# Where the operands of the last matrix product are made: eleven pairs beside one projection, or spread over three

## The chip, the cores and the metric

The kernel runs on one core of one Trainium2 chip. The metric is device time in microseconds (us) of one execution; the median of several executions is compared. A second number, the span, comes from a profiled execution and reaches from its first to its last instruction.

## What is computed

The reference is one layer of a diffusion block over 1024 tokens of width 1024, in fp32:

```python
h = modulate(rmsnorm(x, g_mix), mod[0], mod[1])
p = h @ w_in                       # f_f, f_b, i, q, og, u, v, ga, gb
o_a = HGRN2 scans of p, both directions (512 wide), gated by silu(og)
o_b = spatial gating of gelu(u), gelu(v)   (512 wide)
merged = sigmoid(ga) * (o_a @ w_pa) + sigmoid(gb) * (o_b @ w_pb)
x = x + mod[2] * (merged @ w_o)
h2 = modulate(rmsnorm(x, g_ffn), mod[3], mod[4])
a, b = split(h2 @ w_up)            # 2816 columns each
x = x + mod[5] * ((silu(a) * b) @ w_down)
out = rmsnorm(x, g_final)
```

`mod` are six vectors of 1024 numbers, each `silu(c) @ w_mod[:, j] + b_mod[j]`. `mod[5]`, the last gate, scales the columns of the last product; the kernel multiplies it into `w_down` instead, before the product.

## The kernel before

**Arithmetic.** Every fp32 operand of a large product is split into a high part (ScalarE, ACT, copies it to the reduced format, L92) and a low part (VectorE, DVE, subtracts, L93); three matmuls (L121 to L123) replace one. The input projection, `w_up` and `w_down` use a seven-product Strassen scheme on top, so sums and differences of blocks of both sides are made as well.

**Stages, in order.** Input projection in 18 pairs of column blocks (loop over `PAIRS`, n = 0 to 17); product with `w_pb` (8 column blocks m, L828); scans of four heads; product with `w_pa` (8 blocks, `branch(w_pa, ...)`, L958); `w_o`; `w_up` in 22 pairs (loop from L1033); `w_down` in six segments.

**The vectors of `mod`.** `mod_sum(j)` loads eight blocks of `w_mod` (512 KB each, into the four `raw` buffers that all weights use) and accumulates them with eight DVE instructions (L668, L670). `mod_rows(j, a, dst)` loads the bias row, sums over the partitions with two matmuls (L681) and adds (L682): `dst` is then the vector, the same in every partition. For j = 5 both happen in the `w_up` loop, after m = 2 and m = 4.

**`down_operands(i)`**, the subject of the change, makes what `w_down` needs for the i-th of eleven pairs of row blocks, a set: two loads of 512 KB (`rawd`, two buffers, L1018 and L1019); two multiplications by `m5` on GpSimd (POOL, L1020 and L1021); four differences on DVE (L1024 to L1028, three of them into `t` tiles, which are `gl` buffers); seven splits on ACT and DVE (`od`); seven stores of 512 KB to DRAM (L1031), issued on SyncE's queue (SP), the queue of nearly all loads. The `w_down` stage loads the results again (`so`). The eleven sets are placed in the `w_up` loop after m = 5, 6, 8, 9, 11, 12, 14, 15, 16, 18, 19.

**Memory.** One pool, `slots`, has NS = 31 tiles of 4 KB in each partition and serves nearly every long-lived tile: operands, `m5`, `moda`, the `od` tiles, the scans' tiles. In the `w_up` stage the right-hand operands G are 28 of them (seven names by four). The `gl` tag has six buffers: the gates `g` and the partial results `pb` of `w_pb` and `w_pa`, and the `t` tiles.

**Order.** Outside the first stage nobody writes the order of an engine's queue by hand. A planner walks all instructions with a time model: the one that comes first in the program goes first when it is ready, and a later one takes its place when it is not. So a position in the program is a priority, not a time. On the chip each queue is in order: ACT, DVE, POOL, PE (TensorE) and SP each stand still behind an instruction that waits.

Of the kernel before, what the change touches and what calls it, by code (L numbers as in the profile page):

```python
# [8 lines left out]
F32 = mybir.dt.float32  # L9
# [3 lines left out]
ALU = mybir.AluOpType  # L13
# [21 lines left out]
H0, H1 = slice(0, HALF), slice(HALF, T)  # L35
# [3 lines left out]
def blk(i):  # L39
    return slice(i * P, (i + 1) * P)  # L40
# [3 lines left out]
def block_kernel(ctx: ExitStack, tc: tile.TileContext,  # L44
# [32 lines left out]
    def gl_(name="gl"):  # L77
        return wp.tile([P, HALF], F32, name=name, tag="gl", bufs=6)
# [159 lines left out]
    def dtile(name, shape=(P, T)):  # L238
        return dram.tile(list(shape), F32, name=name)
# [3 lines left out]
    Id = [dtile(f"Id{t}", (P, HALF)) for t in range(TT)]  # L243
    Vd = [dtile(f"Vd{t}", (P, HALF)) for t in range(TT)]
    m2d = dtile("m2d")
    PBd = [dtile(f"PBd{m}") for m in range(KT)]
    X1d = [dtile(f"X1d{t}") for t in range(TT)]
    Gd = [dtile(f"Gd{m}", (P, 2, T)) for m in range(NFF // 2)]
# [143 lines left out]
    with tc.manual_schedule():  # L392
# [22 lines left out]
        a = mods_x(1)  # L415
# [245 lines left out]
    def mod_sum(j):  # L661

        a = slot("moda")
        for k in range(KT):
            raw = raw_()
            load(out=raw, in_=w_mod[blk(k), j * D:(j + 1) * D])
            if k == 0:
                dve.tensor_scalar(a, raw, sc[:, k, 0:1], None, op0=ALU.mult)  # L668
            else:
                dve.scalar_tensor_tensor(a, raw, sc[:, k, 0:1], a, op0=ALU.mult, op1=ALU.add)  # L670
        return a
# [62 lines left out]
    for n, (ka, fa, kb, fb) in enumerate(PAIRS):  # L734
        p_ = early[n] if n < len(early) else in_pair(n).head()
        if n == len(PAIRS) - 1:
            sg4 = slot("sg4", (P, 2, HALF))
            wsr, wsT = sg4[:, 0, :], sg4[:, 1, :]
            bsb = slot("bsb")[:, :HALF]
            load(out=wsr.rearrange("p (g s) -> p g s", s=P), in_=w_s[0].rearrange("g t s -> t g s"))  # L740
            load(out=bsb, in_=b_s.rearrange("a g t -> a (g t)").broadcast_to([P, HALF]))
        X, c12, c21, c22 = p_.rest(turn_ws if n == len(PAIRS) - 1 else None)
        if n == 0:
            with tc.issue_after(t_done.ins):
                for t in range(4):
                    vnorm(4 + t, vlate[t], dve)
        if ka[0] == "q":
            q = slot("q")
            act.copy(q[:, H0], X)
            pool.tensor_copy(q[:, H1], c12)  # L750
            for s, z in ((H0, c21), (H1, c22)):
                sg = gl_("sg")
                sig = after(lambda: act.activation(sg, z, AF.Sigmoid))
                pool.tensor_tensor(z, z, sg, op=ALU.mult)
                store(out=pd[kb][:, s], in_=z)
            table_use[0] = sig
            continue
        if ka[0] == "ff":
            e = ev_()
            zs = (e, c12, c21, c22)  # L760
            for z, src in zip(zs, (X, c12, c21, c22)):
                sig = after(lambda: act.activation(z, src, AF.Sigmoid))
            table_use[0] = sig
            gates(ka[1], zs, q)
        else:
            e = ev_()
            act.activation(e, X, fa)
            todo = ((ka, AF.Copy, H0, e), (ka, fa, H1, c12), (kb, fb, H0, c21), (kb, fb, H1, c22))
        for key, fn, s, z in (todo if ka[0] != "ff" else ()):
            if fn != AF.Copy:  # L770
                last_act = act.activation(z, z, fn)
            store(out=pd[key][:, s], in_=z)
        if n in (11, 13):
            ma = mod_sum({11: 3, 13: 4}[n])
        if n in (12, 14):
            mod_cols({12: 3, 14: 4}[n], ma)
        if n == 15:
            store(out=m2d, in_=mod_sum(2))
        if n == 7:
            act.activation(EA, EA, AF.Exp)  # L780
            E = EA.rearrange("p j (c i) -> p j c i", i=2)
            XA, GA, HA = (const.tile([P, 8, 8, 2], F32, name=nm) for nm in ("XA", "GA", "HA"))
            AP = const.tile([P, 8, 8], F32, name="AP")
            dve.memset(XA, 1.0)
            for dr in range(2):
                d_ = slice(4 * dr, 4 * dr + 4)
                a, b = (0, 1) if dr == 0 else (1, 0)
                Ea, Eb = E[:, d_, :, a], E[:, d_, :, b]
                X_ = XA[:, d_, :, 0]
                dve.tensor_tensor(X_, Ea, Eb, op=ALU.mult)  # L790
                dve.tensor_tensor(AP[:, d_, :], X_, X_, op=ALU.mult)
                dve.tensor_copy(GA[:, d_, :, a], Ea)
                dve.tensor_tensor(GA[:, d_, :, b], X_, Ea, op=ALU.mult)
                dve.tensor_copy(HA[:, d_, :, b], Eb)
                dve.tensor_tensor(HA[:, d_, :, a], X_, Eb, op=ALU.mult)
    dve.scalar_tensor_tensor(A2, modc[:, 4, :], 1.0, cols[:, C_GF:C_GF + 8], op0=ALU.add, op1=ALU.mult)


    V = [slot("V", (P, 2, HALF)) for _ in range(4)]
# [17 lines left out]
    def branch(w, m, src, gate, fin):  # L817
        o = wop(load_cols(w, m * P, 4))
        for h_ in range(2):
            g_ = gl_("g")  # L820
            load(out=g_, in_=pd[gate, m][:, HS[h_]])
            ps = psum()
            for k in range(4):
                mm3(ps, hl(o, blk(k)), hl(src[h_][k]), k == 0, k == 3)
            dve.tensor_tensor(g_, ps, g_, op=ALU.mult)
            fin(h_, g_)

    for m in range(KT):  # L828
        branch(w_pb, m, OB, "gb", lambda h_, g_: store(out=PBd[m][:, HS[h_]], in_=g_))

    scT = [slot(f"scT{d}", (P, NP, P)) for d in range(2)]
    for d in range(2):
# [119 lines left out]
    for m in range(KT):  # L952
        def fin(h_, g_):
            b_ = gl_("pb")
            load(out=b_, in_=PBd[m][:, HS[h_]])
            pool.tensor_tensor(g_, g_, b_, op=ALU.add)
            M[h_][m] = split_into(op_slot("M"), g_)
        branch(w_pa, m, OA, "ga", fin)  # L958
        if m == 3:
            mod_rows(2, ma, m2)  # L960

# [44 lines left out]
                combine(F0[k][0], zs[0], F0[k][1], zs[1], k, G)  # L1006

    SEG = [([0], [1])] + [([4 * i + 2, 4 * i + 3], [4 * i + 4, 4 * i + 5]) for i in range(5)]
    DPAIRS = [(ka, kb) for a, b in SEG for ka, kb in zip(a, b)]
    MADE_AT = {5 + 16 * i // 11: i for i in range(len(DPAIRS))}

    def down_operands(i):
        ka, kb = DPAIRS[i]
        ra, rb = (wp.tile([P, T], F32, name="rawd", tag="rawd", bufs=2) for _ in range(2))
        load(out=ra, in_=w_down[blk(ka), :])  # L1018
        load(out=rb, in_=w_down[blk(kb), :])  # L1019
        pool.tensor_tensor(ra, ra, m5, op=ALU.mult)  # L1020
        pool.tensor_tensor(rb, rb, m5, op=ALU.mult)  # L1021
        x11, x12, x21, x22 = ra[:, H0], ra[:, H1], rb[:, H0], rb[:, H1]
        t1, t3, t4 = (gl_("t") for _ in range(3))
        dve.tensor_tensor(t1, x12, x11, op=ALU.subtract)  # L1024
        dve.tensor_tensor(t3, x22, x12, op=ALU.subtract)
        t2 = x12
        dve.tensor_tensor(t2, x22, t1, op=ALU.subtract)
        dve.tensor_tensor(t4, x21, t2, op=ALU.subtract)  # L1028
        for nm, v in (("B11", x11), ("T1", t1), ("T3", t3), ("T2", t2), ("B22", x22), ("B21", x21), ("T4", t4)):
            o = split_into(op_slot("od"), v)  # L1030
            load(out=Od[nm, i], in_=o.bitcast(F32))  # L1031

    for m in range(NFF):  # L1033
        X, c12, c21, c22 = (early[m] if m < len(early) else up_pair(m).head()).rest()
        e = ev_()
        act.activation(e, X, AF.Silu)
        dve.tensor_tensor(e, e, c21, op=ALU.mult)
        store(out=Gd[m // 2][:, m % 2, H0], in_=e)
        act.activation(c12, c12, AF.Silu)
        pool.tensor_tensor(c12, c12, c22, op=ALU.mult)  # L1040
        store(out=Gd[m // 2][:, m % 2, H1], in_=c12)
        if m == 2:
            ma = mod_sum(5)
# [196 lines left out]
```

## Time and profile before

| what | us |
|---|---|
| median of 3 executions | 1568.43 |
| lowest, highest | 1560.66, 1570.03 |
| profiled execution, its own time | 1572.1 |
| its span | 1570.2 |
| PE, DVE, ACT, POOL busy in the span | 1459.1, 1178.9, 726.7, 684.1 |

In the trace the last input pairs run to about 580 us, `w_pb` to 632, the scans to 703, `w_pa` to 760, `w_o` and its norms to about 860 (the first `w_up` products overlap them), `w_up` to about 1346, `w_down` to the end. Busy times of stretches show how full each engine is; PE's matmuls are pipelined, so the number of matmuls in a stretch says more of its pace than its busy time.

### The profile page before, as it was taken

The numbers are of one execution on the slowest core, as the hardware profiler recorded it, in microseconds if no ns is written. First come the engines' busy times: TensorE is split into PE (matmuls) and PEld (weight loads), VectorE is DVE, ScalarE is ACT, GpSimd is POOL, SyncE is SP. The second block draws the span as 40 slices with busy tenths as digits, with TensorE's granted clock in tenths as the row PEclk, the third lists the DMA queues.
The fourth block names the chain that finished last, engine by engine and source line by source line (L and its number), as shares of the span: only waits on it lengthen the run. The fifth ranks groups of instructions, "written<-read, shape, count | busy, mean of one in ns | idle before, by whom it ended". The sixth has DMA issues, their size and how long they took to land. (4 is left out here: it accounts for less than half of the span.)

```text
span 1570.2 us, 19218 instructions
## 1 busy us (share of the span) xinstructions
PE 1459.1 (93%) x6574; PEld 1182.2 (75%) x6574; DVE 1178.9 (75%) x1642; ACT 726.7 (46%) x1214; POOL 684.1 (44%) x441
## 2 busy tenths in 40 slices
PE   6799979999999999999999899988888899999997
PEld 5677757777788787986888677766766688778886
DVE  5797898988867657775646997888988744578787
ACT  5345545676533331343254523433343334577645
POOL 2663564443233214343314555555564531444356
PEclk9899989999999999999999999999999899999999
DMA  9685302333677577623644263767677724599832
GB/s 304 221 295 161 93 27 81 130 126 114 209 240 227 176 257 270 237 81 119 230 148 161 67 194 115 253 235 268 243 258 256 273 87 141 188 343 355 300 121 107
DMA packets 210963, 302.78 MB, mean 193 GB/s; under 512 B 11857, under 2 KB 132274, under 8 KB 210866
## 3 DMA queue, kind: packets, MB, share of 16 engines
q1 hardware_dynamic: 185954, 253.84, 49.1%
q10 hardware_dynamic: 24912, 47.72, 8.2%
q8 instruction: 51, 0.84, 0.2%
q14 instruction: 46, 0.38, 0.1%
HBM read 211.34 MB, written 90.18 MB: 192 GB/s over the span
## 5 line engine op out<-in xcount | busy, mean ns | idle before, releaser
L93 DVE TENSOR_TENSOR op<-raw,op 128x512 fp32r<-128x512 f32 x200 | 180.5, 907 | 87.0 <-ACT op L92 86.1
L92 ACT CAST op<-raw 128x512 fp32r<-128x512 f32 x216 | 131.7, 620 | 169.7 <-PE acc L123 112.1
L121 PE MATMUL acc<-T,op 128*128 128x512 f32 x408 | 164.9, 405 | 22.4 <-DVE u L188 18.7
L121 PE MATMUL aux<-T,op 128*128 128x512 f32 x408 | 163.8, 402 | 19.1 <-DVE u L188 10.1
L93 DVE TENSOR_TENSOR op<-st,op 128x512 fp32r<-128x512 f32 x160 | 161.0, 1008 | 10.8 <-ACT op L92 9.2
L122 PE MATMUL acc<-T,op 128*128 128x512 f32 x408 | 164.8, 404 | 3.9 <-DVE T L93 3.8
L123 PE MATMUL acc<-T,op 128*128 128x512 f32 x408 | 163.8, 402 | 1.9 <-DVE op L93 1.9
L122 PE MATMUL aux<-T,op 128*128 128x512 f32 x408 | 162.7, 399 | 2.3 <-DVE T L93 2.3
L123 PE MATMUL aux<-T,op 128*128 128x512 f32 x408 | 161.9, 397 | 0.3 <-DVE op L93 0.3
L92 ACT CAST op<-st 128x512 fp32r<-128x512 f32 x160 | 97.9, 618 | 116.3 <-PE aux L123 37.2
L181 POOL TENSOR_TENSOR st<-raw 128x512 f32<-128x512 f32 x40 | 63.9, 1597 | 173.7 <-DMA raw<-in_w_in_dram 90.5
L121 PE MATMUL aux<-B,op 128*128 128x512 f32 x306 | 120.4, 394 | 10.1 <-DVE u L190 9.6
L195 POOL TENSOR_TENSOR st<-raw,st 128x512 f32<-128x512 f32 x40 | 59.3, 1482 | 159.8 <-DVE op L93 143.7
L121 PE MATMUL acc<-B,op 128*128 128x512 f32 x306 | 122.0, 399 | 6.3 <-DVE u L190 4.7
L122 PE MATMUL acc<-B,op 128*128 128x512 f32 x306 | 120.8, 395 | 0.0
L123 PE MATMUL acc<-B,op 128*128 128x512 f32 x306 | 120.6, 395 | 0.0
L123 PE MATMUL aux<-B,op 128*128 128x512 f32 x306 | 119.2, 390 | 0.6 <-DVE op L1155 0.4
L122 PE MATMUL aux<-B,op 128*128 128x512 f32 x306 | 119.4, 390 | 0.0
L121 PEld LDWEIGHTS acc<-T,op 128*128 128x128 f32 x408 | 79.3, 194 | 44.6 <-DVE u L188 21.9
L121 PEld LDWEIGHTS aux<-T,op 128*128 128x128 f32 x408 | 78.4, 192 | 41.0 <-DVE u L188 13.6
L122 PEld LDWEIGHTS acc<-T,op 128*128 128x128 f32 x408 | 79.8, 196 | 21.8 <-DVE T L93 5.4
L123 PEld LDWEIGHTS acc<-T,op 128*128 128x128 f32 x408 | 79.6, 195 | 19.2 <-DVE op L93 2.6
(365 smaller groups left out, 3601.7 us busy)
## 6 DMA issues: line engine op xcount, KB each, us to landing
raw<-in_w_in_dram SPq DMA_DIRECT2D x60, 512.0 KB, 4.9
raw<-in_w_up_dram SPq DMA_DIRECT2D x46, 512.0 KB, 4.2
OdT<-od SPq DMA_DIRECT2D x44, 512.0 KB, 3.6
so<-OdT SPq DMA_DIRECT2D x44, 512.0 KB, 5.6
OdB<-od SPq DMA_DIRECT2D x33, 512.0 KB, 3.5
so<-OdB SPq DMA_DIRECT2D x33, 512.0 KB, 6.0
raw<-in_w_mod_dram SPq DMA_DIRECT2D x32, 512.0 KB, 4.1
rawd<-in_w_down_dram SPq DMA_DIRECT2D x22, 512.0 KB, 5.2
```

The costliest lines, as they stand in the source:

```text
L92: (act.copy if hi_eng is act else hi_eng.tensor_copy)(h, v)
L93: t_last[0] = lo_eng.tensor_tensor(l, v, h.bitcast(F32), op=ALU.subtract)
L121: pe.matmul(ps, lh, rh, start=first, stop=False, skip_group_check=cont)
L122: pe.matmul(ps, lh, rl, start=False, stop=False, skip_group_check=cont)
L123: pe.matmul(ps, ll, rh, start=False, stop=last, skip_group_check=cont)
L181: pool.tensor_tensor(s1, a21, a22, op=ALU.add)
L195: pool.tensor_tensor(s4, a12, s2, op=ALU.subtract)
```

## The change

The last gate's vector is made in the input projection: `mod_sum(5)` after pair 16, `mod_rows` after pair 17, and the result stays in a slot and is also stored to DRAM (`m5d`). `down_operands` moves ahead of `w_pb`, takes the vector as an argument, and is called after m = 1 and 4 of `w_pb` (sets 0 and 1), after m = 1, 3 and 5 of `w_pa` (sets 2 to 4) and after m = 3, 6, 9, 12, 15 and 18 of `w_up` (sets 5 to 10). `last_gate()` loads the vector again for `w_pa` and for `w_up`. One of a set's two multiplications goes from POOL to DVE.

```diff
+    m5d = dtile("m5d")
...
-        if n in (11, 13):
-            ma = mod_sum({11: 3, 13: 4}[n])
+        if n in (11, 13, 16):
+            ma = mod_sum({11: 3, 13: 4, 16: 5}[n])
...
+        if n == 17:
+            m5 = slot("m5")
+            mod_rows(5, ma, m5)
+            store(out=m5d, in_=m5)
...
+    def last_gate():
+        z = slot("m5")
+        load(out=z, in_=m5d)
+        return z
+
+    def down_operands(i, m5):
...
+        dve.tensor_tensor(ra, ra, m5, op=ALU.mult)
+        pool.tensor_tensor(rb, rb, m5, op=ALU.mult)
...
         branch(w_pb, m, OB, "gb", lambda h_, g_: store(out=PBd[m][:, HS[h_]], in_=g_))
+        if m in (1, 4):
+            down_operands(m // 3, m5)
...
         branch(w_pa, m, OA, "ga", fin)
+        if m == 0:
+            m5 = last_gate()
+        if m in (1, 3, 5):
+            down_operands(2 + m // 2, m5)
...
-    MADE_AT = {5 + 16 * i // 11: i for i in range(len(DPAIRS))}
...
-        pool.tensor_tensor(ra, ra, m5, op=ALU.mult)
-        pool.tensor_tensor(rb, rb, m5, op=ALU.mult)
...
-        if m == 2:
-            ma = mod_sum(5)
-        if m == 4:
-            m5 = slot("m5")
-            mod_rows(5, ma, m5)
-        if m in MADE_AT:
-            down_operands(MADE_AT[m])
+        if m == 1:
+            m5 = last_gate()
+        if m >= 3 and m % 3 == 0 and m <= 18:
+            down_operands(4 + m // 3, m5)
```

## Rows read from the trace of the kernel before

**Rows 1.** Page: busy us (share of the span) and instructions, two engines

```profile
PE 1459.1 (93%) x6574; PEld 1182.2 (75%) x6574; DVE 1178.9 (75%) x1642; ACT 726.7 (46%) x1214; POOL 684.1 (44%) x441
```

**Rows 2.** Stretches, w_up: length, PE, PEld, DVE, ACT, POOL busy (instructions), PE clock, DMA, GB/s

```profile
880.00:900.00 20.00, 15.80 (x56) 11.18 (x54) 19.76 (x21) 11.23 (x20) 11.41 (x7) 0.83 0.19 56
900.00:918.94 18.94, 18.18 (x79) 14.72 (x80) 18.94 (x25) 6.15 (x11) 3.93 (x2) 1.00 0.63 198
...
968.56:996.72 28.16, 28.16 (x125) 23.29 (x125) 22.67 (x26) 10.88 (x20) 14.32 (x9) 1.00 0.57 198
...
1065.51:1237.59 172.08, 147.81 (x595) 116.32 (x594) 148.96 (x169) 67.39 (x120) 92.87 (x50) 0.94 0.73 256
1237.59:1254.77 17.18, 13.67 (x54) 10.82 (x53) 10.40 (x15) 5.54 (x10) 7.54 (x6) 0.90 0.86 307
1254.77:1273.58 18.81, 18.81 (x85) 15.58 (x84) 9.29 (x13) 5.73 (x11) 6.39 (x6) 1.00 0.30 92
```

**Rows 3.** POOL in order of time: ends of pairs (L1040), starts of sets (L1020)

```profile
968.56 1.30 POOL L1040 TENSOR_TENSOR m<-m,u 128x512 f32<-128x512 f32 x1
969.81 2.42 POOL L1020 TENSOR_TENSOR rawd<-rawd,m 128x1024 f32<-128x1024 f32 x1
...
1219.07 2.83 POOL L1020 TENSOR_TENSOR rawd<-rawd,m 128x1024 f32<-128x1024 f32 x1
...
1237.59 1.73 POOL L1040 TENSOR_TENSOR m<-m,u 128x512 f32<-128x512 f32 x1
```

**Rows 4.** The tile od: who waited for its stores (us, times), and stores' landing

```profile
  ACT od L92: 105.2, 49
...
DMA to landing us min/median/max: 2.6/3.6/8.2
```

**Rows 5.** DVE in order of time beside one POOL multiplication, within w_up

```profile
1149.37 1.17 DVE L1024 TENSOR_TENSOR t<-rawd 128x512 f32<-128x512 f32 x1
1150.46 2.89 DVE L93 TENSOR_TENSOR op<-st,op 128x512 fp32r<-128x512 f32 x1
1153.28 0.68 DVE L93 TENSOR_TENSOR od<-rawd,od 128x512 fp32r<-128x512 f32 x1
```

**Rows 6.** Groups by line and shape, 860 to 1300: busy us, mean ns, idle before

```profile
L670 DVE SCALAR_TENSOR_TENSOR moda<-raw,sc,moda 128x1024 f32<-128x1024 f32 x7 | 9.3, 1333 | 0.0
```

**Rows 7.** DVE in order of time, input projection: ends of pairs 10, 14 (L200)

```profile
441.04 0.68 DVE L200 TENSOR_TENSOR m<-aux,m 128x512 f32<-128x512 f32 x1
...
520.64 0.68 DVE L200 TENSOR_TENSOR m<-aux,m 128x512 f32<-128x512 f32 x1
```

**Rows 8.** Stretches from the last input pair to w_pa, columns as in Rows 2

```profile
560.00:580.00 20.00, 19.75 (x101) 16.63 (x100) 9.85 (x15) 7.12 (x12) 0.89 (x1) 1.00 0.86 263
580.00:610.00 30.00, 27.99 (x136) 21.68 (x135) 22.11 (x27) 6.72 (x11) 15.90 (x10) 1.00 0.71 247
610.00:650.00 40.00, 40.00 (x263) 34.96 (x262) 25.63 (x38) 8.28 (x16) 12.76 (x6) 1.00 0.99 356
650.00:703.00 53.00, 52.18 (x439) 46.88 (x438) 41.92 (x70) 21.96 (x42) 25.11 (x14) 1.00 0.26 92
703.00:760.00 57.00, 53.14 (x232) 41.74 (x231) 32.85 (x42) 18.57 (x32) 23.52 (x18) 0.97 0.44 145
```

**Rows 9.** Page: DMA issues: count, KB each, us to landing

```profile
OdT<-od SPq DMA_DIRECT2D x44, 512.0 KB, 3.6
...
rawd<-in_w_down_dram SPq DMA_DIRECT2D x22, 512.0 KB, 5.2
```

**Rows 10.** Waits from 600 to 640, three engines: us in total, times, longest

```profile
DVE g L825 <- DMA g<-gb: 7.2, 4, 3.2
...
POOL kd L847 <- DMA kin<-ki: 18.8, 2, 12.6
...
SPq L821 <- DMA PBd<-g: 20.6, 5, 11.9
```

**Rows 11.** Groups by line and shape, 580 to 640: columns as in Rows 6

```profile
L848 DVE TENSOR_TENSOR kx<-kin,XA 128x1024 f32<-128x1024 f32 x2 | 2.4, 1221 | 1.3 <-DMA kin<-ki 1.3
```

**Rows 12.** Waits from 700 to 770: DVE and SP, columns as in Rows 10

```profile
DVE g L825 <- DMA g<-ga: 6.0, 3, 3.2
...
SPq L821 <- POOL g L956: 36.3, 7, 29.7
```

More of the change, by code (lines that the diff above doesn't have):

```diff
@@ L796, in block_kernel @@
     dve.scalar_tensor_tensor(A2, modc[:, 4, :], 1.0, cols[:, C_GF:C_GF + 8], op0=ALU.add, op1=ALU.mult)
+    SEG = [([0], [1])] + [([4 * i + 2, 4 * i + 3], [4 * i + 4, 4 * i + 5]) for i in range(5)]
+    DPAIRS = [(ka, kb) for a, b in SEG for ka, kb in zip(a, b)]
+    def last_gate():
[3 more added lines that the diff above has]
+    def down_operands(i, m5):
+        ka, kb = DPAIRS[i]
+        ra, rb = (wp.tile([P, T], F32, name="rawd", tag="rawd", bufs=2) for _ in range(2))
+        load(out=ra, in_=w_down[blk(ka), :])
+        load(out=rb, in_=w_down[blk(kb), :])
+        dve.tensor_tensor(ra, ra, m5, op=ALU.mult)
+        pool.tensor_tensor(rb, rb, m5, op=ALU.mult)
+        x11, x12, x21, x22 = ra[:, H0], ra[:, H1], rb[:, H0], rb[:, H1]
+        t1, t3, t4 = (gl_("t") for _ in range(3))
+        dve.tensor_tensor(t1, x12, x11, op=ALU.subtract)
+        dve.tensor_tensor(t3, x22, x12, op=ALU.subtract)
+        t2 = x12
+        dve.tensor_tensor(t2, x22, t1, op=ALU.subtract)
+        dve.tensor_tensor(t4, x21, t2, op=ALU.subtract)
+        for nm, v in (("B11", x11), ("T1", t1), ("T3", t3), ("T2", t2), ("B22", x22), ("B21", x21), ("T4", t4)):
+            o = split_into(op_slot("od"), v)
+            load(out=Od[nm, i], in_=o.bitcast(F32))
     V = [slot("V", (P, 2, HALF)) for _ in range(4)]
@@ L1006, in block_kernel @@
                 combine(F0[k][0], zs[0], F0[k][1], zs[1], k, G)
-    SEG = [([0], [1])] + [([4 * i + 2, 4 * i + 3], [4 * i + 4, 4 * i + 5]) for i in range(5)]
-    DPAIRS = [(ka, kb) for a, b in SEG for ka, kb in zip(a, b)]
-    MADE_AT = {5 + 16 * i // 11: i for i in range(len(DPAIRS))}
[L1015 to L1019, printed above, removed]
-        pool.tensor_tensor(ra, ra, m5, op=ALU.mult)
-        pool.tensor_tensor(rb, rb, m5, op=ALU.mult)
[L1022 to L1031, printed above, removed]
     for m in range(NFF):
```

## Prediction

> **What bounds the kernel now.** I read the page's busy times first: PE 93%, DVE 75% [rows 1]. The average decides nothing, since the stages differ, so the stretches by stage come next. In `w_up` they tell the story. Once the sets are done, a pair takes 18.81 us, PE is busy throughout and DVE for 9.29 us. While sets are made, seven pairs take 172.08 us, 24.58 us each, DVE is busy 148.96 us, and the granted clock is 0.94 on average [rows 2]. POOL's order in time gives the rhythm: each pair carries one set. The first set starts at 969.81 us, right after the pair that ends at 968.56 us; the last at 1219.07 us, in the pair that ends at 1237.59 us, though the program places it four pairs later [rows 3]. So the planner pulls sets forward as soon as they are ready; what the text spaces, the queues pack.
>
> The price of a set follows. The eleven pairs from 968.56 to 1237.59 us take 269.0 us and carry eleven sets. At 18.81 us they would take 206.9. That is 62.1 us more; the next pair, 17.18 us, gives 1.6 back [rows 2, 3]. **60.5 us for eleven sets, 5.5 us each.** In DVE time a set costs (148.96 − 7 × 9.29) / 7 = 12.0 us [rows 2], so a pair with a set is 21.3 us of DVE work against 18.81 us of PE work. DVE is the bound there, and the remaining 3.3 us are waits: ACT stood 105.2 us before `od` casts, in 49 waits, until an `od` store had landed [rows 4]. G holds 28 of 31 slots and `m5` one; two are left for `od`.
>
> **The change part by part.** *Sets that leave `w_up`.* Five of eleven: −5 × 5.5 = −27.5 us, if the six that stay are again packed one to a pair. I count on that, since `m5` is read back early in the loop and nothing else holds the sets. Bounds: packed into the first pairs, where DVE is full (19.76 of 20 us, then 18.94 of 18.94) [rows 2], a set could cost its whole 12.0 us instead of 5.5, +6.5; spread out, see the second rival.
>
> *`mod_sum(5)` leaves `w_up`.* Seven accumulations of 1.33 us and one multiplication, some 10 us of DVE [rows 6], go from exactly that full stretch. I take 0, because set 5 (12.0 us) will move in; −10 is the bound if it doesn't.
>
> *`mod_sum(5)` in the input projection.* Four pairs from 441.04 to 520.64 us carry two such sums and take 79.6 us [rows 7]; without them 4 × 18.81 = 75.2 [rows 2]. So 2.2 us a sum: **+2.2** (0 to 4.4). Its eight loads of 512 KB share four `raw` buffers and SP's queue with the last weights; that is in the 2.2. The two matmuls and the bias load only change place. Before the last pair, `moda`, `sg4` and `bsb` and the scans' start state want four slots beside H's 28, one more than there are; the pair's first product frees four, so I take 0 (up to one product of seven, 2.7 us).
>
> *Reading `m5d` back.* A store and two loads of 512 KB, each landing in 3.6 to 5.2 us by the like rows [rows 9], off the path: 0. SP's wait for the vector's slot is the one place where loads could queue behind it.
>
> *The swap of one multiplication to DVE.* DVE pays 1.22 us for 128x1024 elements [rows 11], POOL is spared 2.83 us [rows 3]. Two-input DVE work beside a POOL multiplication is slow: the split at 1150.46 us takes 2.89 us, the next one alone 0.68 [rows 5]. If the spared POOL time gives such a delay back, DVE gains 2.21 and pays 1.22, −1.0; if not, +1.2. I take 0 a set, bounds −6 and +7 for the six sets of `w_up`. The Trainium skill (GPSIMD Engine Reference, Key points) says that GpSimd shares its SBUF interfaces with VectorE, with contention where a VectorE instruction has two SBUF inputs. The trace agrees; by this rule the swap would be the −6 end, by counting instructions the +7 end.
>
> *Two sets beside `w_pb`.* A set moves nine transfers of 512 KB [rows 9], 4.72 MB, at the 356 GB/s of the fullest stretch [rows 8] 13.3 us; two sets 26.5. From 560 to 703 us DMA has 51 us free and DVE 43 us [rows 8], against 26.5 and 24.0 needed: in sum it fits, lower bound 0. But from 610 to 650 us DMA is at 0.99 [rows 8], and its loads are wanted: POOL waits 18.8 us for `kin`, DVE 7.2 us for `gb` [rows 10]. Only 11.5 us of DMA time are free before 610 us, so up to 15 us of `w_pb`'s and the scans' loads land that much later, and PE, which is full there, has nothing else: upper bound 15. Queued behind an `od` store that waits for DVE stand, on SP, the `gb`, `kin` and `qin` loads. I take **+7**, about the middle, since today's waits don't reach PE.
>
> *Three sets beside `w_pa`.* DVE is busy 32.85 of 57 us [rows 8]; three sets make 68.9, 11.9 over. PE idles some 4 us there already, DMA is at 0.44 [rows 8], and sets may slip into `w_o`: lower bound 0. Upper bound 16.5, as dear as in `w_up`. I take **+7**.
>
> The sum: −27.5 + 2.2 + 7 + 7 = −11.3 us. Against the profiled execution, 1572.1 us (span 1570.2), that is 1560.8; that execution lay 3.7 above the median, so I forecast **1557** for the median.
>
> **The rivals.** *First, the moved sets are free.* The waits of ACT for landing stores [rows 4], 9.6 us a set, come from two free slots. Beside `w_pa`, OA holds 8 slots, M grows from 0 to 16, and three vectors take 3: 4 to 20 are free. If the slots, not DVE, set the price, both +7 vanish: −25.3, 1543 us. Against it: DVE alone is over PE's time. The Trainium skill (Perfetto Trace Analysis, Identifying Performance Opportunities) says that the same gap coming back on the engine that should be saturated can mean too little SBUF for the next tile. By that rule this rival is the case; the trace shows the gap once a pair, and DVE beside it.
>
> *Second, the six sets stay apart as written*, one to three pairs: 39.9 us of DVE against 56.4 of PE, so a set would cost perhaps 1 us. −60.5 + 6 + 2.2 + 14 = −38.3, 1530 us. Against it stands the last set that ran four pairs early [rows 3].
>
> *Third, DVE work costs the same wherever it goes*: five sets at 5.5 us again, +27.5. The gain is used up: +2.2, 1571 us. For it: DVE is busy 58 to 79% in those stages too [rows 8].
>
> *Fourth, slower: the `gl` buffers.* A set's `t` tiles hold three of six. A half block of `w_pa` holds two (`g`, `pb`); sixteen pass in 57 us, 3.6 us each, and loads already wait for buffers: SP 36.3 us for POOL's addition in `w_pa`, 20.6 us for the store in `w_pb`; DVE 6.0 us for `ga` [rows 8, 10, 12]. With half the buffers the pace halves while the `t` tiles are held, so a set costs half its hold. If it is held for as long as a set takes in `w_up`, 24.6 us, five sets cost 61.5: −27.5 + 2.2 + 61.5 = +36.2, 1605 us. It decides from a hold of 10 us on, where five halves are 25 us. Against it: a set needs only 12.0 us of DVE, and with free slots nothing stretches it.
>
> **How the numbers follow.** Chances: forecast 0.42 (its own range 1549 to 1565), first rival 0.17, second 0.11, third 0.18, fourth 0.12. The range 1536 to 1580 takes in the forecast, the first and the third rival and leaves out most of the second and of the fourth, 0.2 together. A measurement can tell about 1%, 15.7 us: faster is below 1552.7, slower above 1584.1. Faster: both first rivals and a quarter of the forecast, 0.38; slower: the fourth and a little more, 0.14; the same 0.48.
>
> **What would show it.** Right: in `w_up`, six pairs of about 24.6 us and the rest near 18.8, the stage 27 us shorter; `w_pb` with the scans and `w_pa` some 7 us longer each, PE waiting there for DVE or for `kin`; a third sum about 40 us after the last in the input projection. Wrong: the first rival shows as stages of the old length with five sets in them; the second as sets three pairs apart; the fourth as `ga` and `gb` loads that wait on SP, and PE on L825. The forecast falls first if the planner brings the moved sets somewhere else, into the scans above all, where DVE is busiest.

## The result, and the profile after

The changed kernel takes 1605.69 us (median of 4, 1602.6 to 1607.9) against 1568.11: the ratio is 1.0241, with an interval of 1.0213 to 1.0268. It is slower by 2.4%, where 1557 us was forecast; the time lies outside the range. The profiled execution spans 1601.6 us, 31.4 more than before.

The page's first part answers [rows 1]: PE has the same work, DVE 23 us less and POOL 35 us less, so the 31.4 us are not busy time of any engine added up.

```profile
PE 1459.0 (91%) x6574; PEld 1185.3 (74%) x6574; DVE 1155.9 (72%) x1653; ACT 726.7 (45%) x1214; POOL 649.2 (41%) x430
```

The stretches of the changed kernel, cut where its stages begin and end (columns as in [rows 2]), answer [rows 2, 8]: the end of the input projection, `w_pb`, the scans, `w_pa`, `w_o`, then three stretches of `w_up`.

```profile
500.00:570.00 70.00, 62.72 (x265) 50.40 (x264) 44.82 (x57) 21.31 (x37) 11.00 (x8) 0.95 0.70 218
591.50:655.00 63.50, 53.25 (x222) 43.65 (x223) 40.92 (x57) 16.14 (x28) 13.03 (x8) 0.89 0.76 273
655.00:743.50 88.50, 75.83 (x611) 68.02 (x609) 63.33 (x98) 28.21 (x55) 43.02 (x21) 0.92 0.54 203
743.50:831.00 87.50, 57.16 (x223) 42.99 (x223) 59.02 (x70) 27.45 (x49) 29.93 (x18) 0.86 0.57 204
831.00:925.00 94.00, 91.36 (x418) 75.17 (x417) 52.86 (x76) 39.44 (x69) 24.20 (x17) 1.00 0.58 207
1030.15:1140.24 110.09, 100.11 (x415) 80.75 (x414) 96.95 (x121) 45.59 (x82) 48.78 (x30) 0.95 0.79 272
1140.24:1154.72 14.48, 14.48 (x65) 12.00 (x64) 10.15 (x13) 5.45 (x10) 7.28 (x6) 1.00 0.68 228
1154.72:1344.90 190.18, 190.18 (x840) 157.48 (x840) 91.34 (x130) 60.80 (x102) 63.94 (x51) 1.00 0.28 85
```

`w_up` did what was hoped, and more. Once the sets are done, ten pairs take 19.0 us each with PE full; five pairs with sets take 22.0 us each. What it won was lost almost twice over elsewhere: beside the 222 to 223 matmuls of `w_pb` and of `w_pa` PE now stands idle 10 and 30 us, and no engine is full there on average. The tile `od` answers [rows 4]: ACT waits half as long for its stores, which land later.

```profile
  ACT od L92: 55.4, 27
...
DMA to landing us min/median/max: 2.6/4.7/8.4
```

The stage lengths of all kernels, in us of each profiled execution: from the first matmul on OB (`w_pb`) to the first on OA (`w_pa`), to the last on OA, to the last on M (`w_o`), and to the last store of `Gd` (`w_up`).

| kernel | V's first matmul at | `w_pb` and scans | `w_pa` | `w_o` | `w_up` | median | ratio (interval) |
|---|---|---|---|---|---|---|---|
| before | 576.8 | 121.8 | 55.5 | 91.3 | 499.1 | 1568.11 | 1 |
| after | 585.1 | 152.0 | 87.2 | 93.9 | 457.7 | 1605.69 | 1.0241 (1.0213 to 1.0268) |
| e1 vector only | 582.5 | 120.1 | 54.8 | 90.7 | 491.0 | 1562.55 | 0.9982 (0.9963 to 1.0) |
| e2 two sets by `w_pb` | 584.8 | 154.9 | 52.0 | 91.2 | 471.3 | 1581.53 | 1.0112 (1.0086 to 1.0138) |
| e3 three sets by `w_pa` | 580.2 | 118.9 | 86.7 | 96.5 | 472.3 | 1583.95 | 1.0126 (1.01 to 1.0152) |
| e4 own `t` buffers | 586.2 | 151.9 | 71.0 | 101.1 | 457.6 | 1595.95 | 1.0204 (1.017 to 1.0237) |
| e5 scans' loads first | 586.9 | 144.9 | 71.8 | 102.5 | 456.8 | 1589.71 | 1.0158 (1.0119 to 1.0197) |
| e6 low parts on POOL | 584.6 | 151.4 | 70.7 | 103.3 | 455.9 | 1594.1 | 1.0188 (1.015 to 1.0226) |
| e7 stores on ACT's queue | 582.5 | 151.1 | 75.6 | 95.9 | 457.7 | 1590.04 | 1.0159 (1.0121 to 1.0196) |
| e8 swap only | 572.4 | 120.6 | 53.3 | 92.0 | 488.1 | 1550.16 | 0.9902 (0.9872 to 0.9933) |
| e9 small stores | 586.4 | 135.8 | 64.5 | 101.5 | 457.0 | 1590.54 | 1.0143 (1.012 to 1.0165) |
| e10 low parts on ACT | 582.3 | 145.3 | 64.9 | 98.8 | 457.7 | 1582.63 | 1.0093 (1.007 to 1.0115) |
| e11 vector and swap | 583.2 | 119.0 | 51.7 | 91.8 | 484.5 | 1558.93 | 0.9945 (0.9924 to 0.9966) |
| e12 vector, both on DVE | 586.7 | 119.7 | 52.3 | 92.3 | 475.9 | 1552.14 | 0.9899 (0.9875 to 0.9923) |
| e13 e9 and e10 | 580.6 | 132.6 | 63.1 | 96.6 | 456.1 | 1579.04 | 1.0076 (1.0053 to 1.0099) |
| e14 both on DVE | 571.7 | 120.4 | 54.5 | 90.7 | 483.4 | 1548.35 | 0.9872 (0.9853 to 0.9891) |

From before to after: input projection +8.3, `w_pb` and scans +30.2, `w_pa` +31.7, `w_o` +2.6, `w_up` −41.4, in sum +31.4. What lies between the first matmuls on V and on OB, and behind `w_up`, cancels out (+1.3 and −1.3).

Each kernel has one profiled execution here, and stages that a run left alone differ too: `w_pb` and the scans take 118.9 to 121.8 us in the seven kernels without sets there, `w_pa` 51.7 to 55.5 in the seven without sets in it. So a difference of some 3 us between two rows of the table says nothing.

### The profile page after: what moved, and what is told of

It is laid out like the page before. It is cut to its first block, busy times and chain, and to the rows that moved or that the text cites. A ratio compares the mean times of both kernels' runs of the same rounds, so it can differ in the third digit from the quotient of the medians.

```text
span 1601.6 us, 19213 instructions
## 1 busy us (share of the span) xinstructions
PE 1459.0 (91%) x6574; PEld 1185.3 (74%) x6574; DVE 1155.9 (72%) x1653; ACT 726.7 (45%) x1214; POOL 649.2 (41%) x430
## 5 line engine op out<-in xcount | busy, mean ns | idle before, releaser
L93 DVE TENSOR_TENSOR op<-raw,op 128x512 fp32r<-128x512 f32 x200 | 165.5, 834 | 122.6 <-ACT op L92 119.6
L121 PE MATMUL acc<-T,op 128*128 128x512 f32 x408 | 162.2, 398 | 11.6 <-DVE u L188 8.1
L122 PE MATMUL acc<-T,op 128*128 128x512 f32 x408 | 162.1, 397 | 3.7 <-DVE T L93 3.6
L123 PE MATMUL acc<-T,op 128*128 128x512 f32 x408 | 161.2, 395 | 1.9 <-DVE op L93 1.9
L93 DVE TENSOR_TENSOR op<-st,op 128x512 fp32r<-128x512 f32 x160 | 138.8, 869 | 15.7 <-ACT op L92 12.7
L121 PE MATMUL acc<-B,op 128*128 128x512 f32 x306 | 119.3, 390 | 0.6 <-ACT m L165 0.6
L123 PE MATMUL acc<-B,op 128*128 128x512 f32 x306 | 119.2, 390 | 0.0
L122 PE MATMUL acc<-B,op 128*128 128x512 f32 x306 | 119.1, 389 | 0.0
L121 PEld LDWEIGHTS aux<-T,op 128*128 128x128 f32 x408 | 78.6, 193 | 37.9 <-DVE u L188 12.8
L121 PEld LDWEIGHTS acc<-T,op 128*128 128x128 f32 x408 | 78.0, 191 | 32.4 <-DVE u L188 10.0
L122 PEld LDWEIGHTS acc<-T,op 128*128 128x128 f32 x408 | 78.1, 192 | 21.4 <-DVE T L93 5.7
L122 PEld LDWEIGHTS aux<-T,op 128*128 128x128 f32 x408 | 78.7, 193 | 20.0 <-DVE T L93 3.9
```

The lines of the kernel that those rows point to most:

```text
L121: pe.matmul(ps, lh, rh, start=first, stop=False, skip_group_check=cont)
L122: pe.matmul(ps, lh, rl, start=False, stop=False, skip_group_check=cont)
L123: pe.matmul(ps, ll, rh, start=False, stop=last, skip_group_check=cont)
```

## The experiments

**Which part of the change loses?** e1 to e3 do one part at a time. e1 makes the vector early and leaves all sets in `w_up`, both multiplications on POOL.

```diff
-        dve.tensor_tensor(ra, ra, m5, op=ALU.mult)
+        pool.tensor_tensor(ra, ra, m5, op=ALU.mult)
# no down_operands in w_pb and w_pa; in w_up the places of before (m = 5, 6, 7, 9, ... 19)
```

> The vector of the last gate is made in the input projection and read back in w_up, as in the changed kernel; all eleven sets stay beside w_up with both multiplications on POOL, as before. Theory A (the loss sits in the stages beside w_pb and w_pa, the gain in w_up): the input projection ends some 8 us later, as it did in the changed kernel (585.1 against 576.8 us at the spatial gating's first product), w_up gives a few us back: 1566 to 1578 us. Rival B (the vector's place alone costs most of the 37 us): 1590 us or more.

The places of before are m = 5, 6, 7, 9, 10, 12, 13, 15, 16, 18 and 19; the list ahead of the prediction has 8, 11 and 14 in place of 7, 10 and 13.

Measured: 0.9982, 1562.55 us, somewhat below the range of theory A and far from B's. The vector's place is not the loss. The input projection is 5.7 us longer than in the profiled execution of before (more against e8 and e14, below) and `w_up` 8.1 us shorter.

e2 moves two sets only, e3 three sets only; the swap stays in both.

```diff
# e2: sets 0 and 1 in w_pb as in the change, none in w_pa, nine in w_up (m = 3, 5, ... 19)
# e3: none in w_pb, sets 0 to 2 in w_pa (m = 1, 3, 5), eight in w_up (m = 3, 5, ... 17)
```

> Sets 0 and 1 beside w_pb as in the changed kernel, the other nine beside w_up, every second pair; one multiplication on DVE. Theory A (each stage pays for its own sets): w_pb and the scans keep the 30 us that they lost, w_pa loses nothing, w_up gives 2 sets x 5.5 us and, if the set's price has fallen with the swap, more: 1575 to 1595 us. Rival B (the loss comes from the three sets in w_pa alone): 1555 to 1568 us.

> Three sets (0 to 2) beside w_pa, none beside w_pb, the other eight beside w_up; one multiplication on DVE. Theory A: w_pa keeps its 32 us, w_pb and the scans lose nothing, w_up gives 3 sets x 5.5 us or more: 1570 to 1590 us. Rival B (w_pa is late only because the sets beside w_pb and the scans' late loads push into it): 1545 to 1565 us.

Measured: 1.0112 and 1.0126, both as theory A had it. Each stage pays for its own sets and for no others: in e2 `w_pb` and the scans take 154.9 us and `w_pa` 52.0; in e3 118.9 and 86.7. The whole change has 152.0 and 87.2. So the two losses are separate, and neither needs the other.

**Is it the `gl` buffers?** e4 takes the `t` tiles of the five moved sets from another tag.

```diff
-        t1, t3, t4 = (gl_("t") for _ in range(3))
+        t1, t3, t4 = ((ev_ if i in (0, 1, 2, 3, 4) else gl_)("t") for _ in range(3))
```

> The changed kernel, but the three differences of sets 0 to 4 lie in ev buffers instead of the six gl buffers that the gates and partial results of w_pb and w_pa use. Theory A (the gl buffers, held by the differences, starve the gates): most of the 30 us in w_pb and the scans and of the 32 us in w_pa comes back, 1545 to 1570 us. Rival B (the queues: stores that wait on SP, loads of the scans behind them, instructions of the sets ahead of the gates' on DVE): nothing comes back, 1598 to 1610 us.

Measured: 1.0204, between the ranges of both theories. By the medians 9.7 us come back of 37.6, by the spans 8.0; the intervals of the two ratios overlap. The waits of the changed kernel from 745 to 835 us (engine and line, what it waited for: us in total, times, longest) show the place. The four lines of 10 us show what it looks like: in the first, DVE is full of one set and PE runs no matmul at all; in the second, DVE is busy for 3 us only and DMA is full.

```profile
ACT M L92 <- POOL g L991: 31.6, 11, 7.4
PE acc L121 <- DVE g L858: 29.6, 6, 12.0
POOL g L991 <- DVE g L858: 29.1, 7, 8.7
```

```profile
774.00:784.00 10.00, 0.00 (x0) 0.00 (x0) 9.51 (x13) 4.55 (x8) 2.37 (x1) 0.60 0.50 170
784.00:794.00 10.00, 7.94 (x24) 6.05 (x24) 3.02 (x5) 1.86 (x3) 2.55 (x2) 0.71 1.03 395
794.00:804.00 10.00, 6.04 (x24) 4.35 (x24) 8.69 (x9) 2.85 (x6) 5.36 (x3) 1.00 0.60 213
804.00:814.00 10.00, 5.14 (x15) 3.84 (x16) 9.85 (x16) 3.18 (x6) 2.30 (x2) 0.83 0.92 342
```

PE's longest wait, 12.0 us, ended with the gate's multiplication at 784.27 us. That one waited last for its own `ga` load, which SP issued at 779.77 us, right after an `od` store of the set (DVE and SP in order of time):

```profile
784.27 0.69 DVE L858 TENSOR_TENSOR g<-acc,g 128x512 f32<-128x512 f32 x1 [0.73 <-DMA g<-ga]
```

```profile
779.36 0.32 SPq L829 DMA_DIRECT2D OdT<-od  x1
779.77 0.38 SPq L854 DMA_DIRECT2D g<-ga  x1
```

With buffers of their own the same wait of PE (e4, 745 to 820 us) is less than half:

```profile
PE acc L121 <- DVE g L858: 13.5, 6, 3.9
```

`w_pa` falls from 87.2 to 71.0, but `w_o` grows from 93.9 to 101.1, since the third set now ends there: of 34.3 us in both stages 9.0 come back. The buffers are a cause, and not the larger part. `w_pb` itself is some 5 us shorter, but after the scans nothing is left of that (151.9 against 152.0). The stretches of e4 in `w_pa` show what is next: DVE is nearly full, and DMA too.

```profile
774.00:784.00 10.00, 6.56 (x23) 4.45 (x21) 9.46 (x9) 2.66 (x5) 6.78 (x3) 0.83 0.77 263
784.00:794.00 10.00, 6.01 (x24) 4.35 (x24) 10.00 (x14) 5.32 (x10) 3.29 (x2) 1.00 0.93 317
794.00:804.00 10.00, 5.79 (x15) 4.37 (x16) 7.67 (x10) 2.50 (x5) 5.00 (x3) 0.69 1.03 401
804.00:814.00 10.00, 8.15 (x27) 6.18 (x27) 9.94 (x14) 3.81 (x7) 2.35 (x3) 0.80 0.94 320
```

**Is it the scans' late loads?** In the changed kernel the first load of `kin`, which the scans' first step needs, is issued behind `w_pb`'s loads and the `od` stores, at 656.44 us; before it was 589.98. POOL waits 44.8 us for such loads, 34.0 of them in one piece, and PE 9.7 us for a product of one. First SP in order of time, then two waits from 660 to 745 us:

```profile
656.44 0.32 SPq L878 DMA_DIRECT2D kin<-ki  x1
```

```profile
POOL kd L882 <- DMA kin<-ki: 44.8, 3, 34.0
...
PE aux L911 <- DVE kx L883: 9.7, 1, 9.7
```

e5 (on top of e4) puts the scans' first loads and their preparation ahead of the `w_pb` loop in the program.

```diff
+    pf = prep(0, 0)
     for m in range(KT):
         branch(w_pb, m, OB, "gb", ...)
...
-    pf, pb_ = prep(0, 0), prep(0, 1)
+    pb_ = prep(0, 1)
```

> As e4_own_t, but the scans' first tiles (the four I tiles and their eight loads, the two score tiles, the loads and products of head 0 forward) stand in the program ahead of the w_pb loop, so that they take slots before the od tiles of sets 0 and 1 do. In e4_own_t the scans' stretch from the last OB to the first OA matmul was 93.6 us against 71.8 before, with the kin load at about 657 us instead of 590. Theory A (the od tiles took the slots, so the scans' loads came late): that stretch falls to 72 to 78 us and the time to 1575 to 1582. Rival B (queue order or DMA traffic of the sets holds the scans up): the stretch stays above 88 us, 1590 to 1600 us.

Measured: `w_pb` and scans 144.9 instead of 151.9, seven of thirty us; the scans' stretch that was to fall to 72 to 78 us is 85. So the late loads are a cause. Whether it was SP's order or missing slots that made them late, e5 doesn't tell, since it changes both. SP, in order, stands behind a store that waits for its split: the changed kernel, SP's waits from 595 to 660 us.

```profile
SPq L829 <- DVE od L93: 26.0, 6, 21.0
```

e7 (on top of e4) therefore issues the stores of sets 0 to 4 from ACT's queue, so that no load stands behind them on SP.

```diff
-            load(out=Od[nm, i], in_=o.bitcast(F32))
+            (store if i < 5 else load)(out=Od[nm, i], in_=o.bitcast(F32))
```

> As e4_own_t, but the od stores of sets 0 to 4 are issued on ACT's queue instead of SP's. In e4_own_t SP stood 23.1 us in one piece behind an od store in w_pb and 14.9 us in eight pieces in w_pa. Theory A (SP's queue delays the gate and scan loads): w_pa falls from 71.2 to 56 to 62 us, w_pb from 58.3 to about 52, 1570 to 1583 us. Rival B (SP's wait has nobody behind it that matters, and ACT now waits instead): 1592 to 1605 us.

Measured: 1590.04 us, between the ranges; `w_pb` and the scans take 151.1, no gain; `w_pa` is 4.6 longer than in e4 and `w_o` 5.2 shorter. But the run didn't take SP's wait away. The stores of `PBd` that free the gates' buffers are in ACT's queue too, and a `gb` load of SP now waits for one of them (e7, SP's waits from 590 to 660 us):

```profile
SPq L854 <- DMA PBd<-g: 32.1, 3, 25.9
```

The first `gb` load goes out at 609.79 us, against 609.16 in the changed kernel, and the first `kin` load only at 650.54. So moving the stores gains nothing, and whether SP's order by itself costs PE anything is not shown.

**Is it DVE's time or DMA's?** e6 (on e4) gives four of seven low parts of sets 2 to 4 to POOL; e10 (on e5) gives all of them to ACT as plain copies, which leaves the subtraction out; e9 (on e5) stores only an eighth of each operand of sets 0 to 4; e13 (on e5) does e9 and e10 for sets 0 to 4. The reads in `w_down` of e9 and e13 differ too and take some 18 us longer there, so only their stages are compared, not their medians.

```diff
# e6
-            o = split_into(op_slot("od"), v)
+            o = split_into(op_slot("od"), v, lo_eng=pool if i in (2, 3, 4) and nm in ("B11", "T3", "B22", "B21") else dve)
# e9, for i < 5
-                load(out=Od[nm, i], in_=o.bitcast(F32))
+                load(out=Od[nm, i][:, 0, :P], in_=o.bitcast(F32)[:, 0, :P])
# e10, for i in (2, 3, 4)
-            o = split_into(op_slot("od"), v)
+                act.copy(o[:, 0, :], v)
+                act.copy(o[:, 1, :], v)
```

> As e4_own_t, but four of the seven low parts of sets 2 to 4 (beside w_pa) are made on POOL instead of DVE. In e4_own_t w_pa took 71.2 us from the first to the last OA matmul against 55.7 before, with DVE busy 75% there. Theory A (DVE's time for the sets stands in front of the gates' multiplications): 3 sets x 4 x 0.68 us = 8 us of DVE leave, w_pa falls to 62 to 66 us, 1586 to 1591 us. Rival B (SP's queue: gate loads stand behind od stores that wait): w_pa stays at 69 to 74 us, 1593 to 1600 us.

> As e5_scan_first, but of each od tile of sets 0 to 4 only a block of 128 columns is stored (64 KB instead of 512), and w_down reads that block eight times over, so that the load there is as large as before. Left out: seven eighths of these operands; the result is another one. Two sets then move 6.4 MB less beside w_pb, three 9.6 MB less beside w_pa. Theory A (DMA traffic is what delays the scans' loads: DMA share 0.98 to 1.04 from 632 to 672 us in e5_scan_first): the stretch from the first OB to the first OA matmul falls from 144.9 us to 122 to 132 us; w_pa, where DVE was over 90% busy for 40 us, stays at 66 to 73 us; 1565 to 1578 us in all. Rival B (the instructions of the sets on ACT and DVE): the first stretch stays above 138 us, 1583 us or more.

> As e5_scan_first, but the seven low parts of sets 2 to 4 (beside w_pa) are made by ACT as plain copies instead of DVE's subtractions. Left out: the subtraction, so the low parts are wrong and the result is another one. DVE loses 21 of its some 36 instructions of the three sets, 14 us or more; ACT gains 13 us, POOL nothing. Theory A (DVE's time holds w_pa up; in e6_low_on_pool the same work on POOL slowed DVE by contention): w_pa falls from 71.8 us to 58 to 64 us, 1577 to 1583 us. Rival B (DMA traffic or buffers hold w_pa up): w_pa stays at 68 us or more, 1587 to 1593 us.

> As e9_small_stores, and in addition the low parts of sets 0 to 4 are plain copies by ACT instead of DVE's subtractions. Left out: seven eighths of the stores of those sets and the subtractions; the result is another one, and w_down reads in another pattern, so only the stages count. In w_pa the small stores took 7 us away (71.8 to 64.5) and the lighter DVE took 7 away (71.8 to 64.9). Theory A (DVE and DMA are two separate limits of the same stretch, once the gl buffers are out of the way): w_pa falls to 55 to 60 us, near the 55.7 of before. Rival B (they are one chain, and either relief is all there is): w_pa stays at 62 to 66 us. From the first OB to the first OA matmul (135.8 us in e9, 121.8 before): A, the sets' DVE work is the rest, 122 to 128 us; B, ACT, whose queue stood 28 us before op casts there, is the rest, and with more work on it the stretch stays at 133 us or more.

Measured in `w_pa` and `w_o` together (e4 172.1, e5 174.3, before 146.8): e6 174.0, e9 166.0, e10 163.7, e13 159.7. On POOL the low parts are worth nothing, as rival B had it. Off DVE onto ACT they give 10.6 us, the stores' bytes 8.3, both 14.6, less than the 18.9 of the two: partly the same waits. In `w_pa` alone e9 takes 64.5 us, e10 64.9 and e13 63.1, which is what e13's rival B (one chain) expected, not the 55 to 60 of two separate limits. The 12.9 us that remain are open. The stretches of e6 and of e10 that hold the three sets, one row each:

```profile
772.00:812.00 40.00, 25.59 (x89) 18.90 (x89) 33.31 (x32) 13.85 (x25) 29.21 (x17) 0.87 0.81 290
```

```profile
768.00:808.00 40.00, 27.54 (x91) 21.04 (x92) 27.47 (x35) 23.88 (x44) 17.73 (x11) 0.80 0.98 373
```

In e6 DVE runs 32 instructions and is still busy 33.3 of 40 us, 1.04 us each, where the four rows of e4 above hold 47 of 0.79 us: with POOL busy 29.2 us beside it, DVE's own take longer (a split of M 1.33 us on average against 0.68). In e10 DVE is down to 27.5 us, and DMA is at 0.98.

In `w_pb` and the scans: e5 144.9, e9 135.8, e13 132.6, before 121.8. The bytes of the stores cost 9.1 us there. The low parts come to 3.2, no more than untouched stages differ by, and 10.8 stay open; e13 lies between the ranges of its two theories. Part of the open time lies at the start: in e13 set 0 still runs between the splits that make `w_pb`'s operands OB, PE waits for them (waits from 586 to 612 us), and is busy 16.4 of the 22 us from 590 us on.

```profile
PE acc L122 <- DVE OB L93: 5.6, 2, 3.3
```

```profile
590.00:612.00 22.00, 16.44 (x63) 12.72 (x63) 18.11 (x18) 4.08 (x7) 11.34 (x7) 0.77 0.44 166
```

**What is the swap worth, and is there a better kernel?** e8 and e14 are the kernel before with one or with both multiplications on DVE; e11 and e12 are e1 with the same.

```diff
# e8 and e14, from the kernel before
-        pool.tensor_tensor(ra, ra, m5, op=ALU.mult)
+        dve.tensor_tensor(ra, ra, m5, op=ALU.mult)
# e14 also
-        pool.tensor_tensor(rb, rb, m5, op=ALU.mult)
+        dve.tensor_tensor(rb, rb, m5, op=ALU.mult)
```

> The kernel before, with one of each set's two multiplications on DVE instead of POOL; nothing is moved. In the changed kernel six sets beside w_up cost the pairs 1030.2 to 1154.7 us (six pairs, 124.6 us) 10 us over six pairs of 19.04, 1.7 us a set, where before a set cost 5.5. Theory A (the swap made the sets cheaper): 11 sets save up to 3.8 us each, 1525 to 1550 us. Rival B (the swap is neutral, the sets are cheap in the changed kernel because they are few and start with PE ahead): 1562 to 1572 us.

> The vector made early as in e1_vector_only and one multiplication of each set on DVE as in e8_swap_only; all eleven sets beside w_up. Theory A (the two gains add, 4 and 16 us, since both lie in w_up and neither is a matter of place): 1543 to 1550 us. Rival B (both relieve the same stretch of DVE, and the second adds nothing): 1550 to 1560 us.

> As e11_vector_and_swap, with the second multiplication on DVE too. Theory A (a POOL multiplication of 2.8 us costs DVE and the operands' path more than DVE's own 1.22 us): a further gain of 5 to 15 us, 1530 to 1545 us. Rival B (DVE is full with one, and the second brings its whole 1.22 us a set): 5 to 13 us more than e11_vector_and_swap, 1550 to 1562 us.

> The kernel before, with both multiplications of each set on DVE and nothing moved; the vector too is made beside w_up as before. e8_swap_only (one multiplication on DVE) was 0.990 of before, e12_both_on_dve with the early vector 0.990 and 7 us under e11. Theory A (each multiplication off POOL saves, and the early vector's place gives nothing): 1538 to 1548 us. Rival B (the second multiplication gives nothing of its own): 1548 to 1556 us.

Measured: 0.9902, 0.9945, 0.9899, 0.9872. e8 and e14 lie at the edge of theory A's range. e11 came out as its rival B had it: the gains of the vector and of the swap don't add. In e12 the second multiplication gives 6.8 us by the medians, as theory A had it, though from a higher level. The swap alone takes 11.0 us off `w_up`, with the early vector 6.5; the second multiplication 4.7 and 8.6 more. e8 and e14 can't be told apart by their intervals, but both beat before and after; e14, 1548.35 us, is the lowest. In e8 some 7 us of the difference of the profiled executions lie before `w_up`, where its program is that of before, so they are no work of the swap; one execution can differ from another by as much.

The stretch of the eleven pairs with sets, in the kernel before and then in e8:

```profile
968.56:1237.59 269.03, 236.79 (x966) 188.03 (x966) 232.27 (x263) 105.60 (x188) 144.49 (x78) 0.95 0.70 246
```

```profile
962.29:1218.58 256.29, 231.79 (x957) 185.91 (x957) 230.93 (x272) 104.00 (x186) 112.40 (x67) 0.95 0.72 255
```

DVE took on eleven multiplications, 1.22 us each in the second row below (13.5 us), and is busy no longer than before: its other instructions became as much shorter, above all the splits of `w_up`'s own operands (busy us and mean ns, before and then e8):

```profile
L93 DVE TENSOR_TENSOR op<-st,op 128x512 fp32r<-128x512 f32 x44 | 53.5, 1217 | 0.0
```

```profile
L93 DVE TENSOR_TENSOR op<-st,op 128x512 fp32r<-128x512 f32 x44 | 43.2, 981 | 0.0
```

Its idle time fell from 36.8 to 25.4 us. Of these 11.4 us, 7.1 are the waits of the first difference for POOL's product of `ra` in the kernel before (DVE's waits there), which are gone in e8:

```profile
DVE t L1024 <- POOL rawd L1020: 7.1, 3, 2.5
```

The groups on the tile `rawd` in e8 (durations in ns: lowest, median, highest):

```profile
L93 DVE TENSOR_TENSOR od<-rawd,od x44: 675/692/2883, 965.1 to 1224.5; 128x512 fp32r<-128x512 f32 x44
...
L1020 DVE TENSOR_TENSOR rawd<-rawd,m x11: 1210/1224/1295, 962.1 to 1202.0; 128x1024 f32<-128x1024 f32 x11
L1024 DVE TENSOR_TENSOR t<-rawd x11: 674/684/1666, 963.5 to 1204.3; 128x512 f32<-128x512 f32 x11
L1021 POOL TENSOR_TENSOR rawd<-rawd,m x11: 2392/2842/2860, 964.5 to 1209.6; 128x1024 f32<-128x1024 f32 x11
L1025 DVE TENSOR_TENSOR t<-rawd x11: 678/1165/1777, 969.1 to 1212.9; 128x512 f32<-128x512 f32 x11
```

The median of the first difference (L1024) is 0.68 us here and was 1.18 before; that of the second (L1025) is 1.17 and was 0.68. So around the differences the delay only moved; the gain lies in the splits of `op`.

## Why the prediction was wrong

**Five sets leave `w_up`, −27.5: right in size.** e11 has the vector and the swap but all eleven sets in `w_up`, 484.5 us; after has 457.7. That is 26.8 us, 5.4 a set. The six that stay are packed as foreseen, the first of them at 975.69 us, before the first pair ends; the second starts at 1018.60 us, the sixth at 1113.72, and the pair in which its second multiplication runs ends at 1140.24 (DVE and POOL in order of time, after).

```profile
1018.60 1.21 DVE L818 TENSOR_TENSOR rawd<-rawd,m 128x1024 f32<-128x1024 f32 x1
...
1113.72 1.23 DVE L818 TENSOR_TENSOR rawd<-rawd,m 128x1024 f32<-128x1024 f32 x1 [0.38 <-DMA rawd<-in_w_down_dram]
```

That the price of 5.5 comes out is in part luck: the sets that stay cost less. Five pairs with sets take 3.0 us more each than pairs without, and the next pair, 14.48 us, gives 4.5 back, some 2 us a set.

**`mod_sum(5)` leaves `w_up`, 0 taken, −10 the bound:** 8.1 us (e1). The set that was to fill its place didn't undo the gain.

**`mod_sum(5)` in the input projection, +2.2, at most 4.4:** too low. V's first matmul comes at 571.7 to 576.8 us in the three kernels with the late vector and at 580.2 to 586.9 in the other thirteen, so by 3.4 us at the least and 12 between the medians (572.4 and 584.6). From 500 to 570 us PE runs 265 matmuls in after, 297 in before and 305 in e8 (the first row below). The price came from pairs 11 to 14 [rows 7] and was carried to the last ones. DMA is at 0.70 there instead of 0.62 and, from 570 us on, at 0.92 (after, second row); but most of the loss lies from 540 to 560 us, where PE runs 59 matmuls in after and 90 in e8 while DMA is at 0.53 and DVE busy for 11.2 of 20 us. So neither is full there, and what makes PE wait there was not tried.

```profile
500.00:570.00 70.00, 67.91 (x305) 55.64 (x304) 42.64 (x55) 23.85 (x41) 10.58 (x8) 1.00 0.62 200
```

```profile
570.00:591.50 21.50, 19.16 (x97) 15.04 (x95) 13.99 (x19) 6.00 (x10) 5.79 (x3) 1.00 0.92 306
```

Early against late vector, with the swap in both, is 1558.93 against 1550.16 (e11, e8): `w_up` gains 3.6 us by it in the profiled executions, and the input projection loses 10.8.

**The swap, 0 taken, bounds −6 and +7 for six sets:** −1.0 a set in e8 (11.0 by eleven), −0.6 beside the early vector (e11). Six sets make −6 to −3.6. That is the end that the delays of [rows 5] gave. By the Trainium skill (GPSIMD Engine Reference, Key points) it is also the end that the shared SBUF interfaces give; the trace agrees: the splits of `op` take 0.98 us on average for 1.22 once POOL has half of the multiplications. The step that failed here is the choice of the middle between the two ends, where [rows 5] lay near one of them.

**Two sets beside `w_pb`, +7, upper bound 15: this step failed.** Measured 30.2 (after), 36 from e11 to e2. The bound was too low because it priced one cost alone, the DMA time that pushes loads back. The runs show two that add up: the late issue of the scans' loads (7 us, e5) and the bytes of the stores (9.1, e9). The low parts (3.2, e13) are within what untouched stages differ by, and 10.8 are open. Sums over 143 us hid it, as "51 us of DMA and 43 of DVE free" was true and useless: a set comes in one piece. The first was in part not even beside `w_pb`: it started at 585.66 us, ahead of the splits that make `w_pb`'s operands OB, and only its own splits came behind them (DVE in order of time, after).

```profile
585.66 1.22 DVE L818 TENSOR_TENSOR rawd<-rawd,m 128x1024 f32<-128x1024 f32 x1
...
587.40 2.23 DVE L822 TENSOR_TENSOR t<-rawd 128x512 f32<-128x512 f32 x1
...
593.52 2.84 DVE L93 TENSOR_TENSOR OB<-mb,OB 128x512 fp32r<-128x512 f32 x2
...
608.04 0.68 DVE L93 TENSOR_TENSOR od<-t,od 128x512 fp32r<-128x512 f32 x1
```

That the planner might bring sets somewhere else was named as what would fell the forecast, but it was looked for in the scans, not ahead of `w_pb`.

**Three sets beside `w_pa`, +7, upper bound 16.5: this step failed too.** Measured 31.7, and 34.3 with `w_o`. The price of a set in `w_up`, 5.5 us, had been taken as the dearest. It is not: there a pair brings 84 matmuls with 9.29 us of DVE work, which leaves DVE 9.5 us for a set; in `w_pa` a set stands between PE and each half block's gate (`g`, L858), and POOL, ACT and M behind it. There a set costs 11 us. That is near the 12.0 us of DVE that it takes, but the runs don't show DVE's time as the whole cause: `t` buffers of their own gave 9.0 of the 34.3 us back (e4), and beyond these the low parts off DVE 10.6 (e10), small stores 8.3 (e9), and e10 and e9 together 14.6 (e13).

**The fourth rival** gave 1605 us, which is the time measured, but not for its reason alone. Its mechanism is real: set 0 held its first `t` buffer from 587.40 us to at least the split at 608.04, over 20 us, twice the 10 us from which it was to decide. Yet with the buffers out of the way only 8 to 10 us come back (e4), not 61.5. The number agreed by chance, and its 0.12 was too little for the side it stood on. The third rival, the same cost everywhere, was nearer to the truth than the forecast, and wrong in its premise as well: a set has no single cost. The first rival fell: ACT's waits for landing stores did halve, but the stages with sets grew by 30 and 32 us. So did the second: the six sets stood one to a pair, not apart.

**The balance by the runs:** −26.8 (sets), −8.1 (`mod_sum` out of `w_up`), −6.5 (swap), +8.3 (input projection), +30.2 (`w_pb` and scans), +34.3 (`w_pa` and `w_o`): +31.4, as the spans have it.

**Still open, but narrowed down:** 10.8 us of `w_pb` and the scans and 12.9 of `w_pa` and `w_o`, which are there with separate `t` buffers, early loads, small stores and no low parts on DVE. PE's rows tell idle time from slower matmuls. Before, and then in e13, `w_pb` with the scans and `w_pa`:

```profile
581.90:703.70 121.80, 118.97 (x826) 102.40 (x824) 88.84 (x133) 36.60 (x69) 52.30 (x27) 1.00 0.60 212
703.70:759.20 55.50, 51.64 (x222) 40.38 (x221) 31.89 (x40) 17.25 (x31) 23.18 (x16) 0.97 0.44 145
```

```profile
586.50:719.10 132.60, 122.71 (x822) 106.38 (x823) 98.55 (x141) 51.42 (x97) 55.53 (x29) 0.95 0.60 215
719.10:782.20 63.10, 55.63 (x223) 43.03 (x222) 41.79 (x45) 31.88 (x59) 28.74 (x17) 0.89 0.48 155
```

In the changed kernel PE stands idle 22.9 of the 152.0 us of `w_pb` and the scans, where it was 2.8 of 121.8: 20 of the 30.2 us are waits, and 10 are longer busy time for the same matmuls, where the granted clock is 0.89 and 0.92 in place of 1.00. In `w_pa` it is 26 and 5 us. In e13 7.1 of the open 10.8 us are idle time, and in `w_pa` and `w_o` 7.1 of 12.9; the other 9.5 are longer busy time. What PE waits for in e13 is DVE: the splits OB 5.6 us (above; 1.4 before), a product of `kin` 2.4, and the gates' multiplication 6.7 us in `w_pa` (3.1 before; waits from 719 to 782.5 us) and 3.8 in `w_o`.

```profile
PE acc L121 <- DVE g L866: 6.7, 2, 3.9
```

Whether the multiplication and the differences of the sets, which e13 leaves on DVE, are what makes these late was not tried.

## What to carry to other kernels

A price read in one stage is not a bound for another: ask what the moved work stands in front of there. Where PE waits for the same engine's queue, take the work's whole time on that engine as a possible price (here 12.0 us of DVE a set; 11 were measured, from several causes). Room counted over a stage (free DVE, free DMA) is worth little if the moved work comes in one piece of some 20 us, holds buffers and slots that the stage's own loop uses, and stands in its in-order queues. And test the small part of a change by itself: here one line, a multiplication on DVE, won 1.0% by itself, and the whole change lost 2.4%.

## What the runs showed of the hardware

The same multiplication of 128x1024 fp32 numbers takes 1.22 us on DVE and 2.84 on POOL, and while POOL runs it, single DVE instructions of 0.68 us take 1.2 to 2.9; eleven of them moved to DVE left DVE's busy time as it was (232.27 and 230.93 us). Where PE had stood still, its granted clock fell: 0.60 from 774 to 784 us in after, with no matmul, and still 0.71 in the next ten, where the first matmuls start 0.43 us apart and those from 790 us on 0.23: the lower and the upper of the clock's two levels. And from 655 to 672 us in after DMA moved 409 GB/s, more than the 356 of the fullest stretch that the prediction had reckoned with.

```profile
655.00:672.00 17.00, 7.28 (x44) 6.28 (x43) 5.70 (x7) 2.06 (x3) 4.74 (x2) 0.70 1.04 409
```
